# A decoder layer on one core: the chunks for the seven-product trick loaded in three pieces, one of them by an accumulating transfer

## The chip, the cores and the metric

The kernel runs on one core of a Trainium2 chip. TensorE (PE) multiplies, ScalarE (ACT), VectorE (DVE) and GpSimd (POOL) work on tiles in the on-chip memory, SyncE (SP) issues most of the transfers from DRAM, and POOL issues some of its own. Every engine takes its instructions strictly in order. The metric is the device time of one execution in microseconds (us).

## The reference

One decoder layer in float32 for 256 tokens of width 2048:

```python
f = swiglu(rms_norm(h, ffn1_pre_g), w_gate1, w_up1, w_down1); h = h + 0.5 * rms_norm(f, ffn1_post_g)
u = rms_norm(h, mix_pre_g); proj = u @ w_in          # attention branch and Mamba-2 branch, gated, merged
h = h + rms_norm(merged @ w_out, mix_post_g)
f = swiglu(rms_norm(h, ffn2_pre_g), w_gate2, w_up2, w_down2); h = h + 0.5 * rms_norm(f, ffn2_post_g)
# swiglu(x, wg, wu, wd) = (silu(x @ wg) * (x @ wu)) @ wd      width 5632
```

## The kernel before

Every product is made with float32 weights that are split on the chip into a high part (`w_hi`, written by ACT, L124) and a rest (`w_lo`, written by DVE, L125). PE then needs three matmuls for one product (L377 to L379 in the gate and up projections): high by high, high by rest, rest by high. The split tiles have four buffers for the form of 1024 columns and two for that of 512.

The width 5632 of a feed-forward block goes in 11 steps j of 512 columns. In each j, `gate_up` walks through eight pairs of 128 input rows, each a chunk of 1 MB with four blocks of weights. In j = 1 to 10 three of the eight pairs (SP = 2, 4, 6) use a trick with seven products instead of eight, on sums of the weight blocks: these are "sum pairs" here, the others "plain pairs". A plain pair takes 24 matmuls of 512 columns, a sum pair 21. Two feed-forward blocks with ten such j each make 60 sum pairs. The order of the pairs in a j alternates: sum, plain, sum, plain, sum, plain, plain, plain (ORDER), or with a plain pair first (ORDER_D, in each j that follows a down projection).

The class `Ahead` fetches the chunk of a sum pair. Its 1 MB lands in one of two buffers (`raw7`, shared with the tag "h"), and POOL makes four sums of 128x512 in a row (L359): three into a tile `wsum` (e, two buffers, tag "xc") and one back into the chunk. `take` hands chunk and sums to `gate_up`, which splits them in four parts that are named after the code here: **a** (`raw[:, 0:2]`), **b** (`e[:, 0:2]`), **d** (`e[:, 2]`, 512 columns) and **c** (`raw[:, 2:4]`, which holds the fourth sum). Since there are two buffers, a chunk can be fetched only when the chunk two before it has been split.

The program text does not fix the order on an engine. A scheduler orders the instructions by priority, and `tc.high_priority(offset=AHEAD)` around the splits and around the fetch of `Ahead` pulls them forward. So d, which has its own two buffers, stands on ACT ahead of splits of the sum pair before it. SP takes the fetches and the loads of the plain pairs (L393, three buffers) in one queue.

Of the kernel before, what the change touches and what calls it, by code (L numbers as in the profile page):

```python
# [25 lines left out]
ALU = mybir.AluOpType  # L26
AX = mybir.AxisListType

P = 128
# [3 lines left out]
S = 512  # L33
EPS = 1e-6
NFF = FF // S
NP = D // (2 * P)
# [3 lines left out]
AHEAD = 300  # L40
# [12 lines left out]
def decoder_layer(ctx: ExitStack, tc: tile.TileContext, x, x_t, cols, rows, post_g, wgu1, wd1, w_in,  # L53
                  w_in_t, w_dt, w_att, w_ssm, w_out, wgu2, wd2, out):
    nc = tc.nc
# [51 lines left out]
    ahead = [AHEAD]  # L107
# [232 lines left out]
    class Ahead:  # L340
# [4 lines left out]
            self.w, self.units, self.made = w, list(units), []  # L345

        def make(self):
            if self.made or not self.units:
                return
            j, p = self.units.pop(0)  # L350


            raw = hpool.tile([P, 4, S], F32, name="raw7", tag="h")
            e = tmp.tile([P, 3, S], F32, name="wsum", tag="xc", bufs=2)
            with tc.high_priority(offset=AHEAD):
                nc.sync.dma_start(raw, self.w[j, p])
                for o, a, b in ((e[:, 0], raw[:, 0], raw[:, 3]), (e[:, 1], e[:, 0], raw[:, 1]),
                                (e[:, 2], raw[:, 1], raw[:, 3]), (raw[:, 3], e[:, 1], raw[:, 2])):
                    nc.gpsimd.tensor_tensor(out=o, in0=a, in1=b, op=ALU.add)  # L359
            self.made.append((raw, e))  # L360

        def take(self):
            self.make()
            return self.made.pop()

    def gate_up(at, w, j, order, sp, coming, rstd, fetch=None, after={}):


        count = {k: len(sp) for k in ("p1", "p5", "p6", "p7")}
        count.update({k: len(sp) + 2 * (NP - len(sp)) for k in ("g0", "u0", "g1")}, u1=2 * (NP - len(sp)))  # L370
        bank, done = {}, dict.fromkeys(count, 0)

        def prod(k, xh, xl, wh, wl):
            if k not in bank:
                bank[k] = psm.tile([P, S], F32, name="gu", tag="m")
            done[k] += 1
            nc.tensor.matmul(bank[k], xh, wh, start=done[k] == 1, stop=False)  # L377
            nc.tensor.matmul(bank[k], xh, wl, start=False, stop=False)  # L378
            nc.tensor.matmul(bank[k], xl, wh, start=False, stop=done[k] == count[k])  # L379

        new = lambda name: tmp.tile([P, S], F32, name=name, tag="t2")
        units = [i for i, p in enumerate(order) if p in sp]
        c = {}
        for i, p in enumerate(order):
            if p in sp:
                raw, e = coming.take()
            else:
                raw = fetch(p) if fetch else None
                if coming:
                    coming.make()  # L390
                if raw is None:
                    raw = raws.tile([P, 4, S], F32, name="raw")
                    nc.sync.dma_start(raw, w[j, p])  # L393
            sl, k0 = at[p]
            if p in sp:
                ah, al = split(raw[:, 0:2], [P, 2, S])
                bh, bl = split(e[:, 0:2], [P, 2, S])
                dh, dl = split(e[:, 2], [P, S])
                ch, cl = split(raw[:, 2:4], [P, 2, S])
                seq = {"p1": (0, ah[:, 0], al[:, 0]), "u0": (6, ah[:, 1], al[:, 1]),  # L400
                       "p5": (3, bh[:, 0], bl[:, 0]), "p6": (4, bh[:, 1], bl[:, 1]), "p7": (5, dh, dl),
                       "g0": (1, ch[:, 0], cl[:, 0]), "g1": (2, ch[:, 1], cl[:, 1])}
                for k in (("p1", "p5", "p6", "p7", "u0", "g0", "g1") if i == units[0] else
                          ("p1", "u0", "p5", "p6", "p7", "g0", "g1")):
                    f, wh, wl = seq[k]
                    prod(k, sl[:, f, 0], sl[:, f, 1], wh, wl)
            else:
                ah, al = split(raw[:, 0:2], [P, 2, S])
                bh, bl = split(raw[:, 2:4], [P, 2, S])
                for b, (wh, wl) in enumerate(((ah, al), (bh, bl))):  # L410
                    for t in range(NT):
                        for q, kind in enumerate("gu"):
                            k = k0 + (q + b) % 2
                            xh, xl = (sl[:, k, part, t * P:(t + 1) * P] for part in range(2))
                            prod(f"{kind}{t}", xh, xl, wh[:, q], wl[:, q])
            if units and i == units[-1]:
                c = {k: new(f"c_{k}") for k in ("g0", "g1", "u0", "u1")}
                nc.scalar.activation(c["g0"], bank["p1"], AF.Copy)
                u2 = new("u2")
                nc.vector.tensor_tensor(out=u2, in0=bank["p6"], in1=c["g0"], op=ALU.add)  # L420
                nc.vector.tensor_tensor(out=c["g1"], in0=bank["p7"], in1=u2, op=ALU.add)
                nc.vector.tensor_tensor(out=c["u0"], in0=bank["p5"], in1=u2, op=ALU.subtract)
                nc.vector.tensor_tensor(out=c["u1"], in0=bank["p5"], in1=c["g1"], op=ALU.subtract)
            if i in after:
                after[i]()
        out = []
        for t in range(NT):
            g, u = bank[f"g{t}"], bank[f"u{t}"]
            if c:
                nc.vector.tensor_tensor(out=c[f"g{t}"], in0=g, in1=c[f"g{t}"], op=ALU.add)  # L430
                g = c[f"g{t}"]
                nc.vector.tensor_tensor(out=c[f"u{t}"], in0=u, in1=c[f"u{t}"], op=ALU.add)
                u = c[f"u{t}"]
            sg = g if c else new("sg")
            nc.scalar.activation(sg, g, AF.Silu, scale=rstd()[:, t:t + 1])
            nc.vector.scalar_tensor_tensor(out=sg, in0=u, scalar=rstd()[:, t:t + 1], in1=sg,
                                           op0=ALU.mult, op1=ALU.mult)
            out.append(sg)
        return out

    def ffn(xo, scale, wgu, wd, gi, h_of, fetch=None):
# [14 lines left out]
        for a, b in groups:  # L456
            hs = []
            for j in range(a, b):
                if j == 0:
                    steps = dict(scale)  # L460

                    def behind(i):
                        if i in steps:
                            rs.append(steps[i]())
                        if i - 1 in SP:
                            xo.sums(i - 1)
                        if i == NP - 1:
                            coming.make()
                    todo.append(gate_up(xo.at0, wgu, 0, range(NP), (), None, lambda: rs[-1], fetch,
                                        {i: lambda i=i: behind(i) for i in range(NP)}))  # L470
                else:
                    todo.append(gate_up(xo.at, wgu, j, order(j), SP, coming, lambda: rs[-1], after={5: flush}))
            last = b == NFF
            if last:
                h = [hpool.tile([P, D], F32, name=f"h{t}", tag="h") for t in range(NT)]
                for t in range(NT):
                    nc.gpsimd.dma_start(h[t], h_of(t))
            if not post:
                post = PostNorm(gi, 0.5)
                f = post.f  # L480

            def final():
                flush()
                return hs[-1]

            lazy = hs + [final]
            for n in range(4):
                if n == 3:
                    coming.make()
                pd = project(lazy, lambda n, c: wd[n, a + c], n, by_token=2 if last and n == 3 else 0)  # L490
                part = f[:, :, n * S:(n + 1) * S]
                if not last:
                    for t in range(NT):
                        if a == 0:
                            nc.scalar.activation(part[:, t], pd[t], AF.Copy)
                        else:
                            nc.vector.tensor_tensor(out=part[:, t], in0=pd[t], in1=part[:, t], op=ALU.add)
                else:
                    def get(t):
                        v = tmp.tile([P, S], F32, name="fsum", tag="t2")  # L500
                        nc.vector.tensor_tensor(out=v, in0=pd[t], in1=part[:, t], op=ALU.add)  # L501
                        return v
                    post.slab(n, get)
# [21 lines left out]
        return inv_rms(s1)  # L525

    def fetch1(p):
        for k in (2 * p, 2 * p + 1):
            if 2 <= k < NP:
                nc.sync.dma_start(xT[:, k], x_t[k])  # L530
        x1.make(p, xT[:, p], C_PRE1)
        return None if p else raw0
# [450 lines left out]
```

## Time and profile before

| | |
|---|---|
| median of 3 runs | 2853.56 us (2853.48 to 2854.42) |
| profiled execution | 2857.27 us, its span 2855.6 us |
| PE busy | 2785.7 us, 98% of the span |
| DVE, ACT, POOL busy | 1961.6, 1432.6, 542.2 us |
| mean granted clock of PE | 0.996 |
| DMA | 541.50 MB, mean 190 GB/s |

An engine's busy time is the time in which one of its instructions runs, waits inside an instruction included. Consecutive matmuls overlap, so that a matmul of 0.39 us does not mean a step of 0.39 us from one to the next. The span runs from the first to the last instruction.

### The profile page before, as it was taken

What the parts mean: (1) busy time and instruction counts of PE and PEld (TensorE: products, weight loads), DVE (VectorE), ACT (ScalarE), POOL (GpSimd) and SP (SyncE); (2) the same over time, 40 slices, a digit from 0 to 9 for tenths busy, and PEclk for the clock granted to TensorE, in tenths of its full rate; (3) what the DMA queues carried; (4) which work ended last, traced back from release to release, by engine and by line L of the source; (5) the groups of instructions that cost most, each with busy time, mean ns of one, the idle gap of its engine ahead of it and who ended that gap; (6) DMA issues with size and microseconds to landing.
All of it is one profiled execution on the core that took longest, in us unless ns stands there. A gap on an engine that the chain in (4) does not pass through costs nothing. (4 is left out here: it accounts for less than half of the span.)

```text
span 2855.6 us, 33775 instructions
## 1 busy us (share of the span) xinstructions
PE 2785.7 (98%) x13120; PEld 2310.1 (81%) x13120; DVE 1961.6 (69%) x2311; ACT 1432.6 (50%) x1822; POOL 542.2 (19%) x377
## 2 busy tenths in 40 slices
PE   7999999999999999999999999999999999999998
PEld 6887787887788888888788888888877887877877
DVE  6857858867777876777765555545567658678576
ACT  5544544545555555555444444444455545445454
POOL 3403305212012120111100000000033224034030
PEclk9999999999999999999999999999999999999999
DMA  6555555545555555545554445555555554545554
GB/s 239 195 194 184 194 186 193 196 177 213 193 199 178 186 183 184 200 162 193 200 183 171 169 176 178 199 193 197 192 206 192 192 192 177 204 179 192 193 187 165
DMA packets 77985, 541.50 MB, mean 190 GB/s; under 512 B 8768, under 2 KB 8912, under 8 KB 14080
## 3 DMA queue, kind: packets, MB, share of 16 engines
q1 hardware_dynamic: 73152, 519.08, 50.7%
q0 software_dynamic: 4528, 20.09, 2.1%
q8 instruction: 103, 1.69, 0.2%
q14 instruction: 58, 0.48, 0.1%
q10 hardware_dynamic: 144, 0.17, 0.0%
HBM read 532.94 MB, written 6.36 MB: 189 GB/s over the span
## 5 line engine op out<-in xcount | busy, mean ns | idle before, releaser
L125 DVE TENSOR_TENSOR w_lo<-raw,w_hi 128x1024 fp32r<-128x1024 f32 x978 | 1265.0, 1305 | 677.9 <-ACT w_hi L124 670.1
L124 ACT ACTIVATE w_hi<-raw 128x1024 fp32r<-128x1024 f32 x978 | 1022.4, 1057 | 901.1 <-PE acc L132 590.8
L130 PE MATMUL acc<-w_hi,slot 128*128 128x512 f32 x1856 | 729.7, 393 | 1.1 <-DVE y L719 0.3
L131 PE MATMUL acc<-w_lo,slot 128*128 128x512 f32 x1856 | 723.1, 390 | 0.0
L132 PE MATMUL acc<-w_hi,slot 128*128 128x512 f32 x1856 | 720.5, 390 | 0.0
L130 PEld LDWEIGHTS acc<-w_hi,slot 128*128 128x128 f32 x1856 | 348.9, 188 | 78.7 <-ACT slot L187 4.6
L131 PEld LDWEIGHTS acc<-w_lo,slot 128*128 128x128 f32 x1856 | 349.0, 188 | 72.8 <-issue 1.0
L171 PE MATMUL acc<-slot,w_hi 128*128 128x512 f32 x1280 | 407.4, 399 | 0.2 <-ACT zs L763 0.2
L132 PEld LDWEIGHTS acc<-w_hi,slot 128*128 128x128 f32 x1856 | 348.7, 188 | 72.7
L377 PE MATMUL gu<-w_hi,slot 128*128 128x512 f32 x928 | 364.4, 394 | 12.7 <-ACT w_hi L124 12.7
L359 POOL TENSOR_TENSOR wsum<-raw 128x512 f32<-128x512 f32 x120 | 196.1, 1654 | 927.1 <-DMA raw<-in_wgu 743.1
L378 PE MATMUL gu<-w_lo,slot 128*128 128x512 f32 x928 | 364.2, 392 | 5.5 <-DVE w_lo L125 5.5
L379 PE MATMUL gu<-w_hi,slot 128*128 128x512 f32 x928 | 363.3, 391 | 0.0
L173 PEld LDWEIGHTS acc<-slot,w_lo 128*128 128x128 f32 x1280 | 240.4, 188 | 56.3
L124 ACT ACTIVATE w_hi<-wsum 128x512 fp32r<-128x512 f32 (+1 forms) x120 | 101.5, 846 | 309.3 <-POOL wsum L359 260.1
L125 DVE TENSOR_TENSOR w_lo<-wsum,w_hi 128x512 fp32r<-128x512 f32 (+1 forms) x120 | 165.0, 1384 | 127.8 <-ACT w_hi L124 127.8
L173 PE MATMUL acc<-slot,w_lo 128*128 128x256 f32 x1280 | 252.6, 278 | 0.0
L377 PEld LDWEIGHTS gu<-w_hi,slot 128*128 128x128 f32 x928 | 175.7, 189 | 49.9 <-ACT w_hi L124 13.2
L378 PEld LDWEIGHTS gu<-w_lo,slot 128*128 128x128 f32 x928 | 175.7, 189 | 44.1 <-DVE w_lo L125 7.6
L379 PEld LDWEIGHTS gu<-w_hi,slot 128*128 128x128 f32 x928 | 175.5, 189 | 36.5
L171 PEld LDWEIGHTS acc<-slot,w_hi 128*128 128x128 f32 x1280 | 196.4, 189 | 3.8 <-issue 2.4
L378 PE MATMUL gu<-w_lo,sums 128*128 128x512 f32 x420 | 168.7, 402 | 28.2 <-DVE w_lo L125 27.6
(226 smaller groups left out, 2172.5 us busy)
## 6 DMA issues: line engine op xcount, KB each, us to landing
raw<-in_wgu SPq DMA_DIRECT2D x175, 1024.0 KB, 4.8
raw<-in_wd SPq DMA_DIRECT2D x88, 1024.0 KB, 4.8
raw<-in_w_in SPq DMA_DIRECT2D x80, 1024.0 KB, 4.8
raw<-in_w_in_t SPq DMA_DIRECT2D x80, 1024.0 KB, 4.7
raw<-in_w_ssm SPq DMA_DIRECT2D x32, 1024.0 KB, 4.7
raw<-in_w_att SPq DMA_DIRECT2D x16, 1024.0 KB, 4.7
raw<-in_w_out SPq DMA_DIRECT2D x16, 1024.0 KB, 4.7
dec<-acsD POOLq DMA_DIRECT2D x16, 512.0 KB, 5.1
```

Of the source, the lines that this page charges most:

```text
L124: nc.scalar.activation(hi[:, js], raw[:, js], AF.Copy)
L125: nc.vector.tensor_tensor(out=lo[:, js], in0=raw[:, js], in1=hi[:, js].bitcast(F32), op=ALU.subtract)
L130: nc.tensor.matmul(ps, xh, wh, start=first, stop=False)
L131: nc.tensor.matmul(ps, xh, wl, start=False, stop=False)
L132: nc.tensor.matmul(ps, xl, wh, start=False, stop=last)
L171: nc.tensor.matmul(ps[f], hi[:, j, wf[f]], sl[:, j], start=b + j == 0, stop=False)
L173: nc.tensor.matmul(ps[f][:, TT:], lo[:, j, wf[f]], sl[:, j, :TT], start=False, stop=b == len(xs) - 1 and j == 3)
L359: nc.gpsimd.tensor_tensor(out=o, in0=a, in1=b, op=ALU.add)
L377: nc.tensor.matmul(bank[k], xh, wh, start=done[k] == 1, stop=False)
L378: nc.tensor.matmul(bank[k], xh, wl, start=False, stop=False)
L379: nc.tensor.matmul(bank[k], xl, wh, start=False, stop=done[k] == count[k])
```

## The change

A chunk is now fetched in three transfers. SP loads the fourth block twice, side by side, into `e[:, 0:2]` (L357, 512 KB) and the first three blocks into `raw` (L358, 768 KB). POOL then issues a transfer that adds the first two blocks from DRAM onto `e[:, 0:2]` (L359). That makes two of the four sums; the two left are made by POOL as before (L360, L361). The sums in e change places, so that d is now the sum of three blocks and p6 and p7 swap roles. `made` may hold two chunks, `make` is called behind the splits of a sum pair, and the calls elsewhere are moved. The splits of the very first chunk (`fetch1`, p = 0) lose their priority.

```diff
             self.w, self.units, self.made = w, list(units), []
 
         def make(self):
-            if self.made or not self.units:
+            if len(self.made) == 2 or not self.units:
                 return
             j, p = self.units.pop(0)
 
 
             raw = hpool.tile([P, 4, S], F32, name="raw7", tag="h")
             e = tmp.tile([P, 3, S], F32, name="wsum", tag="xc", bufs=2)
+            src = self.w[j, p]
             with tc.high_priority(offset=AHEAD):
-                nc.sync.dma_start(raw, self.w[j, p])
-                for o, a, b in ((e[:, 0], raw[:, 0], raw[:, 3]), (e[:, 1], e[:, 0], raw[:, 1]),
-                                (e[:, 2], raw[:, 1], raw[:, 3]), (raw[:, 3], e[:, 1], raw[:, 2])):
-                    nc.gpsimd.tensor_tensor(out=o, in0=a, in1=b, op=ALU.add)
+                nc.sync.dma_start(e[:, 0:2], src[:, 3:4].broadcast_to([P, 2, S]))
+                nc.sync.dma_start(raw[:, 0:3], src[:, 0:3])
+                nc.gpsimd.dma_start(e[:, 0:2], src[:, 0:2], accum_op=ALU.add)
+                nc.gpsimd.tensor_tensor(out=e[:, 2], in0=e[:, 0], in1=raw[:, 1], op=ALU.add)
+                nc.gpsimd.tensor_tensor(out=raw[:, 3], in0=e[:, 2], in1=raw[:, 2], op=ALU.add)
             self.made.append((raw, e))
 
         def take(self):
             self.make()
-            return self.made.pop()
+            return self.made.pop(0)
...
                 raw = fetch(p) if fetch else None
-                if coming:
-                    coming.make()
                 if raw is None:
...
                 ch, cl = split(raw[:, 2:4], [P, 2, S])
+                coming.make()
                 seq = {"p1": (0, ah[:, 0], al[:, 0]), "u0": (6, ah[:, 1], al[:, 1]),
-                       "p5": (3, bh[:, 0], bl[:, 0]), "p6": (4, bh[:, 1], bl[:, 1]), "p7": (5, dh, dl),
+                       "p5": (3, bh[:, 0], bl[:, 0]), "p7": (5, bh[:, 1], bl[:, 1]), "p6": (4, dh, dl),
                        "g0": (1, ch[:, 0], cl[:, 0]), "g1": (2, ch[:, 1], cl[:, 1])}
-                for k in (("p1", "p5", "p6", "p7", "u0", "g0", "g1") if i == units[0] else
-                          ("p1", "u0", "p5", "p6", "p7", "g0", "g1")):
+                for k in (("p1", "p5", "p7", "p6", "u0", "g0", "g1") if i == units[0] else
+                          ("p1", "u0", "p5", "p7", "p6", "g0", "g1")):
...
-                        if i == NP - 1:
+                        if i >= NP - 2:
                             coming.make()
...
             for n in range(4):
-                if n == 3:
-                    coming.make()
...
     def fetch1(p):
+        ahead[0] = AHEAD if p else 0
```

On ACT, in the first j behind a down projection of the first feed-forward block, before (`raw7_1783` and `wsum_1784` are a chunk and its sums, `wsum_1872` the sums of the next chunk, `raw_1790` and `raw_1878` are plain pairs):

```order
L124 ACTIVATE w_hi_1792<-raw_1790 128x1024
L124 ACTIVATE w_hi_1796<-raw_1790 128x1024
L124 ACTIVATE w_hi_1824<-raw7_1783 128x1024
L124 ACTIVATE w_hi_1828<-wsum_1784 128x1024
L124 ACTIVATE w_hi_1962<-wsum_1872 128x512
L124 ACTIVATE w_hi_1836<-raw7_1783 128x1024
L124 ACTIVATE w_hi_1880<-raw_1878 128x1024
```

The same engine and place with the change (`raw7_1687`/`wsum_1688` and the next chunk's `wsum_1770`):

```order
L124 ACTIVATE w_hi_1799<-raw_1797 128x1024
L124 ACTIVATE w_hi_1803<-raw_1797 128x1024
L124 ACTIVATE w_hi_1831<-raw7_1687 128x1024
L124 ACTIVATE w_hi_1969<-wsum_1770 128x512
L124 ACTIVATE w_hi_1835<-wsum_1688 128x1024
L124 ACTIVATE w_hi_1843<-raw7_1687 128x1024
L124 ACTIVATE w_hi_1887<-raw_1885 128x1024
```

The split d of the next chunk (128x512) stood between b and c of the pair at hand; now it stands between a and b. Over the kernel, d stands directly ahead of b at 1 place before and at 27 with the change, ahead of c at 37 and 12.

On SP, in the same stretch, before:

```order
L356 DMA raw7_1871<-in_wgu1 128x2048
L393 DMA raw_2005<-in_wgu1 128x2048
L356 DMA raw7_1998<-in_wgu1 128x2048
L393 DMA raw_2084<-in_wgu1 128x2048
L393 DMA raw_2172<-in_wgu1 128x2048
```

With the change:

```order
L393 DMA raw_2012<-in_wgu1 128x2048
L357 DMA wsum_1848<-in_wgu1 128x2x512
L358 DMA raw7_1847<-in_wgu1 128x1536
L393 DMA raw_2091<-in_wgu1 128x2048
L393 DMA raw_2179<-in_wgu1 128x2048
```

Each fetch is two entries instead of one, at the same place between the loads of plain pairs (L393). At the very start of the kernel SP had one fetch of 1 MB ahead of the first piece of x; now two L358 (768 KB each) stand there.

On POOL, at the first two chunks, before:

```order
L359 TENSOR_TENSOR wsum_544<-raw7_543 128x512 x2
L359 TENSOR_TENSOR wsum_544<-wsum_544,raw7_543 128x512
L359 TENSOR_TENSOR raw7_543<-wsum_544,raw7_543 128x512
L104 TENSOR_TENSOR pre_rstd_470<-rs_v_471,mhalf_99 128x2
L359 TENSOR_TENSOR wsum_623<-raw7_622 128x512 x2
```

With the change:

```order
L359 DMA wsum_494<-in_wgu1 128x1024
L104 TENSOR_TENSOR pre_rstd_477<-rs_v_478,mhalf_99 128x2
L360 TENSOR_TENSOR wsum_494<-wsum_494,raw7_493 128x512
L361 TENSOR_TENSOR raw7_493<-wsum_494,raw7_493 128x512
L359 DMA wsum_523<-in_wgu1 128x1024
```

The power that makes the scale of x (`pre_rstd`) stood behind the four sums of the second chunk; now it stands behind the issue of the second accumulating transfer, and the two sums left come after it.

## Rows read from the trace of the kernel before

**Rows 1.** Page: busy us, share of the span, instructions.
```profile
PE 2785.7 (98%) x13120; PEld 2310.1 (81%) x13120; DVE 1961.6 (69%) x2311; ACT 1432.6 (50%) x1822; POOL 542.2 (19%) x377
```
**Rows 2.** Waits of PE: engine, waited for, us in total, times, longest.
```profile
PE gu L378 <- DVE w_lo L125: 33.1, 37, 2.5
```
**Rows 3.** Waits of all engines, same columns.
```profile
POOL wsum L359 <- DMA raw<-in_wgu: 743.1, 50, 84.6
...
ACT w_hi L124 <- POOL wsum L359: 260.1, 59, 5.6
```
**Rows 4.** Timeline of one fetch: start us, us, engine, operation, [idle before].
```profile
238.84 0.33 SPq L356 DMA_DIRECT2D raw<-in_wgu  x1
...
243.90 2.52 POOL L359 TENSOR_TENSOR wsum<-raw 128x512 f32<-128x512 f32 x2 [6.22 <-DMA raw<-in_wgu]
...
246.46 0.64 ACT L124 ACTIVATE w_hi<-wsum 128x512 fp32r<-128x512 f32 x1 [4.75 <-POOL wsum L359]
247.00 2.00 ACT L124 ACTIVATE w_hi<-raw 128x1024 fp32r<-128x1024 f32 x2
247.13 1.10 DVE L125 TENSOR_TENSOR w_lo<-wsum,w_hi 128x512 fp32r<-128x512 f32 x1 [3.82 <-ACT w_hi L124]
...
248.16 4.59 DVE L125 TENSOR_TENSOR w_lo<-raw,w_hi 128x1024 fp32r<-128x1024 f32 x3
...
250.54 0.33 SPq L356 DMA_DIRECT2D raw<-in_wgu  x1
```
**Rows 5.** Timeline of PE early on, two matmuls six apart.
```profile
19.08 0.39 PE L378 MATMUL gu<-w_lo,slot 128*128 128x512 f32 x1
...
20.44 0.39 PE L378 MATMUL gu<-w_lo,slot 128*128 128x512 f32 x1
```
**Rows 6.** Timeline of PE: three of its waits in one group of j.
```profile
250.53 0.50 PE L378 MATMUL gu<-w_lo,sums 128*128 128x512 f32 x1 [0.91 <-DVE w_lo L125]
...
279.38 0.50 PE L378 MATMUL gu<-w_lo,sums 128*128 128x512 f32 x1 [1.60 <-DVE w_lo L125]
290.84 0.50 PE L378 MATMUL gu<-w_lo,sums 128*128 128x512 f32 x1 [0.94 <-DVE w_lo L125]
```
**Rows 7.** Timeline of PE: its waits at the two feed-forward blocks' starts.
```profile
12.25 1.29 PE L377 MATMUL gu<-w_hi,slot 128*128 128x512 f32 x2 [12.25 <-ACT w_hi L124]
...
40.62 0.50 PE L378 MATMUL gu<-w_lo,slot 128*128 128x512 f32 x1 [1.54 <-DVE w_lo L125]
...
68.45 0.50 PE L377 MATMUL gu<-w_hi,sums 128*128 128x512 f32 x1 [2.04 <-ACT sg L435]
...
2139.30 0.50 PE L378 MATMUL gu<-w_lo,slot 128*128 128x512 f32 x1 [1.02 <-DVE w_lo L125]
...
2144.86 0.80 PE L378 MATMUL gu<-w_lo,slot 128*128 128x512 f32 x1 [2.50 <-DVE w_lo L125]
```
**Rows 8.** Transfers: issuing queue, count, KB each, median us from issue to landing.
```profile
raw<-in_wgu SPq DMA_DIRECT2D x175, 1024.0 KB, 4.8
...
dec<-acsD POOLq DMA_DIRECT2D x16, 512.0 KB, 5.1
...
out<-h SPq DMA_DIRECT2D x8, 256.0 KB, 2.2
```
**Rows 9.** The 16 transfers of 512 KB that POOL issues at L694.
```profile
L694 POOL DMA_DIRECT2D dec<-acsD x16: 547/564/686, 842.4 to 1358.0; - x16
...
DMA to landing us min/median/max: 3.7/5.1/6.1
```
**Rows 10.** Source line L359, POOL: count, duration ns min/median/max, first and last start.
```profile
L359 POOL TENSOR_TENSOR wsum<-raw x120: 1272/1300/4334, 30.4 to 2766.6; 128x512 f32<-128x512 f32 x120
```
**Rows 11.** Source line L125, DVE, same columns.
```profile
L125 DVE TENSOR_TENSOR w_lo<-raw,w_hi x978: 1204/1225/3436, 12.2 to 2837.8; 128x1024 fp32r<-128x1024 f32 x196
```
**Rows 12.** Stretches: us; PE, PEld, DVE, ACT, POOL busy (x); PEclk, DMA share, GB/s.
```profile
69.50:73.00 3.50, 3.50 (x10) 2.71 (x9) 3.50 (x3) 2.66 (x4) 3.42 (x3) 0.51 0.23 33
...
2144.80:2148.30 3.50, 3.44 (x8) 2.78 (x9) 3.50 (x5) 0.75 (x1) 0.00 (x0) 0.51 0.67 225
```

## The prediction

> **What bounds the kernel now.** I read the page first: PE is busy for 2785.7 of 2855.6 us, so everything the kernel can win is the 70 us in which PE sits idle [rows 1]. Then the waits of PE: apart from the start, the one large item is the matmul that waits for a `w_lo`, 33.1 us in 37 waits [rows 2]. Following that back through the waits of all engines: DVE waits for ACT, and ACT's 260.1 us of waiting for POOL's sums, 59 times, is what holds it up; POOL itself mostly waits for the chunk to land [rows 3]. So the chain of one fetch is what matters, and the timeline has it [rows 4]. SP issues a fetch at 238.84; the sums begin at 243.90; ACT, which stood at split d of that chunk, goes on at 246.46, 7.62 us after the issue. Only then come c of the pair at hand (ACT 247.00), d's rest (DVE 247.13) and c's rest (248.16), and the buffer that this frees lets SP issue the next fetch at 250.54. The reader is to see a loop: fetch, sum, split, free the buffer, fetch. It takes 250.54 - 238.84 = 11.70 us, of which DVE and ACT have 4.08.
>
> PE's work in such a turn is a sum pair and a plain pair, 21 + 24 = 45 matmuls. Six matmuls take 20.44 - 19.08 = 1.36 us, 0.227 each [rows 5], so 10.2 us. The loop is 1.5 us longer than the work, and PE waits 0.91 at 250.53 [rows 6]. A waiting matmul also hides 0.39 - 0.227 = 0.16 of its wait, so PE loses 1.07; the other 0.43 come out of splits made ahead. At 279.38 and 290.84 the same [rows 6]. At the starts of the two blocks lie 1.54 + 1.02 + 2.50 = 5.06 of the 33.1 [rows 7]; in the steady j remain 28.0 us in 34 waits, with the hidden 34 x 0.16 = 5.5 about 33 us.
>
> **The change, part by part.** *Two pairs ahead* frees nothing: the chunk has two buffers before and after, the fetch before already goes out when the chunk two before it is split, and SP's order shows the fetches at the same places. I cost it at 0. What changes is the loop.
>
> (1) The fetch becomes a chain of two transfers. The 512 KB of L357 have no row on SP's queue: 256 KB out take 2.2 and 1 MB in takes 4.8 [rows 8], I take the middle, 3.6 with the wake-up of POOL. Then POOL issues the accumulating transfer and it lands after L. No such transfer is in the trace. The nearest rows are POOL's 512 KB of L694: 3.7 at least, 5.1 in the median, 6.1 at most [rows 9]. Below nothing the cost of adding can't be, so 3.7 is the lower end; at the upper end the destination is read as well, 512 KB more, which between 256 KB and 1 MB costs (4.8 - 2.2) / 1.5 = 1.7, so 7.8. L694's transfers go in twos, and the second has 512 KB of its twin in front of it, about what the second read would be: between median and maximum, L = 5.6.
>
> (2) One sum instead of two before d: 1.3 [rows 10]. The sums removed, 2 x 60 x 1.3 = 156 us of POOL, are off PE's path except through this place, and against them stand 60 issues of 0.56 [rows 9].
>
> (3) On ACT d now stands ahead of b at 27 places, not of c. The wait at d so holds up b, which PE needs earlier, and b frees `e` for the next L357. From d to that: d's step 247.00 - 246.46 = 0.54, b's high part 1.05 (two such take 2.00 at 247.00), its rest 1.21 [rows 4, 11], and 0.25 for d's rest on DVE in between: 3.05.
>
> The loop with the change is 3.6 + L + 1.3 + 3.05 = 8.0 + L, with 0.05 for two wake-ups. Against 10.2 us of work and 0.43 in hand PE loses L - 2.6 a turn, 3.0 at L = 5.6. I count one full turn in each of the 20 j with sums, and the other 7 places (the second in a j behind a down projection, whose loop has already stretched) at a third: 22.3 turns. That gives 22.3 x 3.0 = 67 us of waiting where 33 are now: +34.
>
> (4) At the starts. The two L358 ahead of x are 512 KB more than the one fetch before, by the same slope 1.7 us later than 12.25 [rows 7]: +1.7; between nothing, if they are passed in the queues, and 2.4. The first splits without priority stand behind two short slot instructions that run while the chunk is still under way: 0. The wait at 68.45 for the scale of x stays: POOL has the power behind the second accumulating issue now, which itself waits for an L357, instead of behind four sums. At the second block's start, 1.02 and 2.50 should go, since POOL has half the sums to make there, and with them the stretch after it in which PE's clock is granted at 0.51 for 3.4 us [rows 12], worth half of that, 1.7: -5.2. Together -3.5.
>
> (5) The DMA queues carry 0.75 MB more for each of 60 chunks, 45 MB on 541.5: the plain pairs' loads have three buffers and I cost it at 0; if that cover goes, a late load costs PE up to the 2.4 us that L357 and L358 occupy longer.
>
> Sum: +34 - 3.5 = +30 us. On the profiled execution's 2857.3 that is 2888; the median of the runs is 3.7 lower, so 2884. With L in between, 22.3 x (L - 2.6) - 36.5: -12 at 3.7, +19 at 5.1, +42 at 6.1, +80 at 7.8.
>
> The Trainium skill, "Collectives: The Full Stack", section "The bandwidth ceiling: the fold count and why AG ≠ RS ≠ AR", says that an add in a DMA engine costs no cycles of its own but needs two source reads on one ring, so such a stream runs at half the rate (1.93 measured there). No run here shows it yet. By that rule the full 1.7 come on top of the median, L = 6.8, and the sum would be +57, 2911.
>
> **The rivals.** *Faster.* The accumulating transfer lands like a lone plain one. For it: the smallest of L694 is 3.7, and its firsts have no twin ahead. Against it: the median is 5.1, and a destination must be read. From L = 4.2 down the sum above is negative. What makes more of it is DVE: POOL's sums slow it, as where d's rest takes 1.10 and three of c's kind take 4.59 instead of 3 x 1.21 [rows 4, 11], and half of them go. At most all steady waits vanish, -33 - 3.5; at L = 3.7 the sum alone gives -12. The middle, -24: 2830.
>
> The Trainium skill, "SBUF — State Buffer", section "Who interferes with whom", has a VectorE instruction with two SBUF inputs and a GpSimd instruction that reads SBUF block each other for whole instructions. The trace agrees: the 4.59 are about 1.0 more than three rests, near one sum's 1.3. By it this rival has its price; the sum above counts only 0.25 of it.
>
> *Clock.* The waits of 2.04 and 2.50 [rows 7] are each followed by 3.5 us at a granted 0.51 [rows 12], that is 1.2 GHz instead of 2.4; 1.60 at 279.38 is not. If 20 waits of about 3 us each bring such a stretch, 20 x 1.7 = 34 come on top: 2918.
>
> *Nothing.* SP's order and the buffers are as before, L lies near 4.2 and the longer chain and the shorter sums cancel: 2854.
>
> **How the numbers follow.** About 0.2% or 5.7 us is what a measurement of this kernel can tell from no change. Forecast, 0.45: 2884, its own range 2866 to 2908 (L from 4.9 to 6.5). Clock or an L near 7: 0.15, 2918. Nothing: 0.08. Faster: 0.32, 2830. So faster 0.32, same 0.08, slower 0.60. The range from 2826 to 2924 leaves out about 1 in 10 at each end.
>
> **What would show it.** L359's time to landing is the first thing to read: 5.6 for the forecast, under 4.2 for the faster rival. Then L357 to L357 across an alternating pair (13.6 against 11.70), ACT's waits for POOL's sums (more than 260.1 us), PE's waits for `w_lo` (about 60 us against 33.1, at 20 to 27 places and near 3 us long), granted clock behind them, first matmul at 13.9. The prediction is wrong if L359 lands fast, if d ends up off the path because b was split long before PE needs it, or if the plain pairs' loads come late beside the accumulating ones.

## The result, and the profile after

The changed kernel takes 3029.5 us (median of 4 runs, 3020.5 to 3035.4) against 2853.7 for the kernel before: ratio 1.0611, 95% interval 1.0598 to 1.0624. It is slower by 176 us. The sign was forecast; 2884 and its range, up to 2924, were far too low.

The page after (busy us, share, instructions; then the DMA queues: packets, MB, share of 16 engines):

```profile
PE 2848.1 (94%) x13120; PEld 2349.2 (78%) x13120; DVE 1873.3 (62%) x2311; ACT 1429.2 (47%) x1822; POOL 365.0 (12%) x317
...
q1 hardware_dynamic: 89472, 534.81, 49.6%
q0 software_dynamic: 13168, 51.55, 7.9%
```

The span is 3028.9 us, 173.3 longer than before. PE's time splits exactly into busy and idle: it is busy 62.4 us longer with the same 13120 matmuls [rows 1], and idle for 180.8 instead of 69.9, 110.9 more. DVE, ACT and POOL are busy for less time than before, so the work of no other engine explains it. The waits (engine, waited for: us, times, longest):

```profile
ACT w_hi L124 <- POOL wsum L360: 448.6, 60, 12.3
POOL wsum L360 <- DMA wsum<-in_wgu: 303.2, 47, 10.4
PE gu L379 <- ACT w_hi L124: 120.1, 33, 14.0
PE gu L380 <- DVE w_lo L125: 32.6, 38, 1.5
PE gu L379 <- ACT sg L436: 6.2, 2, 5.7
```

Without the first matmul's 14.0, PE waits 144.9 us here; before it was 33.1 [rows 2] and some small ones. ACT's 260.1 us at split d [rows 3] have become 448.6. One fetch, to be laid beside [rows 4] (timeline: start us, us, engine, operation, idle before):

```profile
252.67 0.38 SPq L357 DMA_DIRECT2D wsum<-in_wgu  x1
253.77 0.33 SPq L358 DMA_DIRECT2D raw<-in_wgu  x1
...
256.04 0.33 SPq L393 DMA_DIRECT2D raw<-in_wgu  x1
...
257.83 0.87 POOL L359 DMA_DIRECT2D wsum<-in_wgu  x1 [6.91 <-DMA wsum<-in_wgu]
265.53 1.25 POOL L360 TENSOR_TENSOR wsum<-wsum,raw 128x512 f32<-128x512 f32 x1 [6.83 <-DMA wsum<-in_wgu]
266.81 1.58 ACT L124 ACTIVATE w_hi<-wsum 128x512 fp32r<-128x512 f32 x2 [11.41 <-POOL wsum L360]
...
268.44 0.79 PE L379 MATMUL gu<-w_hi,sums 128*128 128x512 f32 x1 [5.30 <-ACT w_hi L124]
...
269.88 0.38 SPq L357 DMA_DIRECT2D wsum<-in_wgu  x1
```

From fetch to fetch 17.21 us instead of 11.70. It reads: 5.16 until POOL issues the accumulating transfer, 7.70 until its landing lets POOL add, 1.28 for the sum, 3.07 for d, b and the freeing of the buffer. ACT stands 11.41 us at d, and b, which PE needs, stands behind it (the x2 at 266.81 is d and b together). PE then waits, and this is what its clock does (stretch; busy us of PE, PEld, DVE, ACT, POOL; granted clock; DMA share; GB/s):

```profile
258.00:265.90 7.90, 5.14 (x23) 3.94 (x21) 0.00 (x0) 0.00 (x0) 1.07 (x2) 1.00 0.79 214
265.90:272.80 6.90, 3.72 (x8) 2.64 (x9) 5.32 (x5) 5.29 (x7) 2.15 (x2) 0.51 0.19 64
272.80:283.00 10.20, 10.03 (x44) 7.93 (x43) 2.24 (x3) 0.67 (x1) 0.98 (x2) 1.00 0.83 240
```

PE has stood since 263.15; from 265.90 it is granted half, 1.2 GHz, the wait of 5.30 ends at 268.44, and work goes on at half speed until 272.80. There are 30 such stretches between the first matmul and the last, 181 us in all; before there were 5, 20.5 us. The transfers (count, KB, median us to landing), with L359's issue and landing in full:

```profile
raw<-in_wgu SPq DMA_DIRECT2D x115, 1024.0 KB, 6.0
...
raw<-in_wgu SPq DMA_DIRECT2D x60, 768.0 KB, 5.2
wsum<-in_wgu SPq DMA_DIRECT2D x60, 512.0 KB, 4.4
wsum<-in_wgu POOLq DMA_DIRECT2D x60, 512.0 KB, 7.0
```
```profile
L359 POOL DMA_DIRECT2D wsum<-in_wgu x60: 847/872/915, 34.9 to 2934.5; - x60
...
DMA to landing us min/median/max: 5.2/7.0/11.2
```

The accumulating transfer lands after 7.0 in the median, not 5.6, and the plain 1 MB loads beside it need 6.0 where they needed 4.8 [rows 8].

The 7.0 is the median of two groups. When 25 of the 60 transfers were issued, a 1 MB load of a plain pair (L393) was on its way, as at 256.04 above; these landed after 7.0 to 11.2, in the median 7.8. The other 35 took 5.5 in the median. PE waits 22 times for more than 2 us at a `w_hi` after the start, and the transfer in front of each of these waits is one of the 25.

### The profile page after: what moved, and what is told of

Read it like the earlier page. It is cut to its first block, busy times and chain, and to the rows that moved or that the text cites. A ratio compares the mean times of both kernels' runs of the same rounds, so it can differ in the third digit from the quotient of the medians.

```text
span 3028.9 us, 33954 instructions
## 1 busy us (share of the span) xinstructions
PE 2848.1 (94%) x13120; PEld 2349.2 (78%) x13120; DVE 1873.3 (62%) x2311; ACT 1429.2 (47%) x1822; POOL 365.0 (12%) x317
## 3 DMA queue, kind: packets, MB, share of 16 engines
q0 software_dynamic: 13168, 51.55, 7.9%
## 5 line engine op out<-in xcount | busy, mean ns | idle before, releaser
L125 DVE TENSOR_TENSOR w_lo<-raw,w_hi 128x1024 fp32r<-128x1024 f32 x978 | 1214.5, 1253 | 688.4 <-ACT w_hi L124 681.2
L379 PE MATMUL gu<-w_hi,slot 128*128 128x512 f32 x928 | 375.0, 405 | 33.5 <-ACT w_hi L124 33.5
L380 PE MATMUL gu<-w_lo,slot 128*128 128x512 f32 x928 | 374.6, 404 | 11.3 <-DVE w_lo L125 11.3
L381 PE MATMUL gu<-w_hi,slot 128*128 128x512 f32 x928 | 372.5, 402 | 0.0
L125 DVE TENSOR_TENSOR w_lo<-wsum,w_hi 128x1024 fp32r<-128x1024 f32 (+1 forms) x120 | 139.9, 1182 | 369.1 <-ACT w_hi L124 369.1
L124 ACT ACTIVATE w_hi<-wsum 128x1024 fp32r<-128x1024 f32 (+1 forms) x120 | 98.5, 841 | 486.2 <-POOL wsum L360 448.6
L379 PE MATMUL gu<-w_hi,sums 128*128 128x512 f32 x420 | 180.6, 430 | 92.7 <-ACT w_hi L124 86.5
L379 PEld LDWEIGHTS gu<-w_hi,slot 128*128 128x128 f32 x928 | 182.1, 196 | 75.5 <-ACT w_hi L124 36.9
L381 PEld LDWEIGHTS gu<-w_hi,slot 128*128 128x128 f32 x928 | 181.5, 196 | 38.9
L380 PE MATMUL gu<-w_lo,sums 128*128 128x512 f32 x420 | 180.0, 429 | 21.4 <-DVE w_lo L125 21.3
```

The lines of the kernel that those rows point to most:

```text
L124: nc.scalar.activation(hi[:, js], raw[:, js], AF.Copy)
L125: nc.vector.tensor_tensor(out=lo[:, js], in0=raw[:, js], in1=hi[:, js].bitcast(F32), op=ALU.subtract)
```

## The experiments

Theory A was: ACT stops at split d of the next chunk; b of the chunk at hand, the buffer that b frees and the next fetch stand behind it; so the whole length of one fetch lies in a loop, and each microsecond that the chain of two transfers adds is paid, with the clock on top. The rivals: the traffic or the software queue (POOL's, which carries L359) holds everything up wherever d stands; or other parts of the change do it. Names in the diffs are those of the changed kernel.

| run | what is different | median us | PE busy | PE idle |
|---|---|---|---|---|
| before | | 2853.7 | 2785.7 | 69.9 |
| x5_before_sums | before's fetch and sums; two ahead, first splits | 2854.7 | 2784.0 | 70.4 |
| x1_pool_sums | the same, sums in the new form | 2881.4 | 2794.5 | 83.8 |
| x2_plain_second | chain of two, no add | 2946.7 | 2819.5 | 113.6 |
| changed kernel | chain of two, add | 3029.5 | 2848.1 | 180.8 |
| x3_d_behind_b | changed, d behind its own b | 2805.9 | 2767.4 | 36.5 |

(Medians; the kernel before has medians between 2853.7 and 2856.4 beside these runs. Busy and idle are of one profiled execution each; that of x2 is the fastest of its runs.)

**Undoing the accumulating transfer**, in two forms:

```diff
-nc.sync.dma_start(e[:, 0:2], src[:, 3:4].broadcast_to([P, 2, S]))
-nc.sync.dma_start(raw[:, 0:3], src[:, 0:3])
-nc.gpsimd.dma_start(e[:, 0:2], src[:, 0:2], accum_op=ALU.add)
+nc.sync.dma_start(raw, src)
 # x1: e0 = r0+r3, e1 = r1+r3, e2 = e0+r1, r3 = e2+r2
 # x5: e0 = r0+r3, e1 = e0+r1, e2 = r1+r3, r3 = e1+r2; p6, p7 as before
```

> The changed kernel with the accumulating transfer undone: one fetch of 1 MB and four sums on POOL again; two chunks ahead, first splits without priority and the order of p5, p7, p6 stay. Theory A (the loss of 176 us is the longer chain of a fetch, L357, L359, L360, that ACT stands and waits for at split d): the time is back within 15 us of before, 2840 to 2870, ACT's waits for POOL's sums near 260 us, PE's near 33 to 45, a landing of the 1 MB at 4.8 us. Theory B (two chunks ahead, the new order of the sums or the first splits cost it): it stays above 2930.

Measured: 2881.4 us, 1.0089 [1.0074, 1.0104], 349.0 us of ACT's waits for POOL. Neither theory's number. The timeline of x1 shows why:

```profile
244.70 2.53 POOL L360 TENSOR_TENSOR wsum<-raw 128x512 f32<-128x512 f32 x2 [6.63 <-DMA raw<-in_wgu]
247.19 1.29 POOL L360 TENSOR_TENSOR wsum<-wsum,raw 128x512 f32<-128x512 f32 x1
248.51 0.63 ACT L124 ACTIVATE w_hi<-wsum 128x512 fp32r<-128x512 f32 x1 [6.13 <-POOL wsum L360]
```

Split d takes `e2`, which the new formula makes of `e0`; on POOL it is the third sum, and ACT goes on at 248.51 when it has ended. In the kernel before d's sum needs the raw chunk alone, stands second, and ACT goes on at 246.46 while POOL begins the third [rows 4]. So the run still had a change in it that I had overlooked. x5 took it out.

> The 1 MB fetch and the four sums on POOL word for word as in the kernel before (d is there the sum of chunks 1 and 3, ready as POOL's second, not third), with p6 and p7 as before; of the change only two chunks ahead and the first splits without priority are left. Theory A: the 27 us that the run with four sums in the new form lost are the third sum, 1.3 us, that d waits for in each loop; without it the time is that of before, 2848 to 2862. Rival (two chunks ahead or the first splits cost the 27): 2875 or more.

Measured: 2854.7 us, 1.0002 [0.9992, 1.0011], as theory A had it. Two chunks ahead and the first splits without priority are together worth nothing here, and one POOL sum of 1.3 us more in front of d costs 27 us.

**The chain without the add.**

```diff
-nc.gpsimd.dma_start(e[:, 0:2], src[:, 0:2], accum_op=ALU.add)
+nc.gpsimd.dma_start(e[:, 0:2], src[:, 0:2])
```

> The changed kernel with L359 as a plain transfer, which overwrites what L357 brought instead of adding to it (so two of the four sums of weights are left out); queue, size, chain and all waits are the same. Theory A with the add's second read as its main price: L359's time to landing falls from 7.0 in the median to 4.5 to 5.5, the loop from 17.2 to about 14.5, the time to 2870 to 2930. If the two reads are all of it: 2860 or less. If the software queue and the chain of two transfers are the price and not the add: L359 still lands at 6.5 or more and the time stays above 2990.

Measured: 2946.7 us, 1.0321 [1.0303, 1.0338]; landing 3.3/4.9/7.8, issue 570 ns. L fell as the theory with the second read had it; the time stayed 17 us above that theory's range, which ended at 2930. One tight turn, that is, one in which a fetch waits for the one before it:

```profile
238.01 0.38 SPq L357 DMA_DIRECT2D wsum<-in_wgu  x1
...
243.18 0.57 POOL L359 DMA_DIRECT2D wsum<-in_wgu  x1 [6.91 <-DMA wsum<-in_wgu]
249.34 1.26 POOL L360 TENSOR_TENSOR wsum<-wsum,raw 128x512 f32<-128x512 f32 x1 [5.59 <-DMA wsum<-in_wgu]
250.63 1.58 ACT L124 ACTIVATE w_hi<-wsum 128x512 fp32r<-128x512 f32 x2 [8.63 <-POOL wsum L360]
...
253.70 0.38 SPq L357 DMA_DIRECT2D wsum<-in_wgu  x1
```

15.69 us, and 6.16 of them for a plain transfer: here too the 26 transfers that were issued with an L393 under way took longer, 6.1 in the median against 4.2 for the other 34. So of the 176 us, 92 come with the chain of two plain transfers (x2 against x5) and 83 with the add. The 27 us of x1 are no part of them: in the changed kernel one sum stands before d, not three.

**Less traffic beside the chain.**

```diff
-nc.sync.dma_start(raw[:, 0:3], src[:, 0:3])
+nc.sync.dma_start(raw[:, 1], src[:, 1])        # splits a and c and the last sum read raw[:, 1] for 0 and 2
```

> The changed kernel, order and chain unchanged, with less traffic beside the chain: L358 brings 256 KB (chunk 1 alone) instead of 768, and the splits a and c read chunk 1 where they would read chunks 0 and 2, so those weights are left out. Theory: 1.6 us of the 17.2 us loop are L357 sharing the DMA engines with L358, and part of L359's 7.6 the same, which the prediction costed at nothing. Then the POOL issue stands at about 4.2 after L357 instead of 5.2, L359 lands in 6 to 6.5 in the median, a loop of 15 to 16, the time 2930 to 2985. Rival (the landing is long by itself, the neighbours do nothing): 3015 or more, L359 still near 7.0.

Measured: 2979.1 us, 1.0430 [1.0415, 1.0446], 50 less than the changed kernel and inside the theory's range; L359 lands after 5.1/6.2/10.1, POOL's issue follows L357 by 4.57 in the median instead of 4.97. So the 512 KB that L358 no longer brings are a part of the price; 123 us of the loss remain, with the loads of the plain pairs still beside the chain.

**The accumulating transfer in halves.**

```diff
-nc.gpsimd.dma_start(e[:, 0:2], src[:, 0:2], accum_op=ALU.add)
+for k in range(2):
+    nc.gpsimd.dma_start(e[:, k], src[:, k], accum_op=ALU.add)
```

> The changed kernel with L359 cut into two accumulating transfers of 256 KB, one for each half; d needs the first only. If the price goes by bytes read and added (7.0 us in the median for 512 KB, 4.9 without the add): the first half lands after 4.5 to 5.5, the loop loses about 2 us, time 2920 to 2980. If it is a fixed price for each transfer, or the traffic around it: the first lands after 6.5 or more, the second issue of 0.9 us comes on top, time 3030 or more.

Measured: 3002.7 us, 1.0518 [1.0502, 1.0534], between the two. The 256 KB land after 3.6/6.7/11.0, the firsts of the pairs after 6.2 in the median, and each is issued in 0.98 us. Half the bytes are far from half the time. Of the 60 firsts, the 30 that were issued with a load of a plain pair under way took 6.5 in the median, the others 3.9; for the whole 512 KB these were 7.8 and 5.5. So the half, too, is long where such a load is under way.

**Split d behind split b of the same chunk.** The order of ACT before the edit reads a8 d9 b8 c8 in such a place (pairs numbered), after it a8 b8 d8 c8.

```diff
-dh, dl = split(e[:, 2], [P, S])
+dh, dl = split(e[:, 2], [P, S], behind=last[0])     # last[0]: b's ACTIVATE
...
-            for i in queue.pop(0) if queue else ():
+            for i in [behind] if behind else queue.pop(0) if queue else ():
                 st.enter_context(tc.issue_after(i.ins))
...
-                nc.scalar.activation(hi[:, js], raw[:, js], AF.Copy)
+                last[0] = nc.scalar.activation(hi[:, js], raw[:, js], AF.Copy)
```

> The changed kernel, accumulating transfer and all, with one thing moved: split d of a chunk is issued behind split b of the same chunk instead of one pair ahead. Theory A (ACT stands at d of the next chunk, and behind it wait b of the chunk at hand, the buffer that b frees, and so the next fetch): one fetch no longer waits for the one before, the 17.2 us loop opens, ACT's waits for POOL's sums fall from 448.6 to under 150, PE's waits at w_hi from 120.1 to under 30, half-speed stretches from 188 us to under 40, and the time falls below 2860, by the work alone perhaps to 2815. Rival (the traffic: 45 MB more and a queue whose packets take twice as long hold up every load, wherever d stands): it stays above 2930. L359 should take its 7 us in both.

Measured: 2805.9 us, 0.9827 [0.9813, 0.9842] of the kernel before, 224 us less than the changed kernel, with every transfer, sum and matmul of it in place. L359's landing is 5.3/7.1/10.9: as slow as ever, and harmless. ACT's waits for that sum are 0.5 us in all, PE's idle time is 36.5, and 10 us are left at half speed.

```profile
ACT w_hi L125 <- POOL wsum L361: 0.5, 2, 0.2
```

The timeline of x3 (its L358, L360, L361 are L357, L359, L360 of the changed kernel):

```profile
250.87 1.58 ACT L125 ACTIVATE w_hi<-wsum 128x1024 fp32r<-128x1024 f32 x2 [1.65 <-PE gu L382]
...
253.87 0.38 SPq L358 DMA_DIRECT2D wsum<-in_wgu  x1
...
258.13 0.87 POOL L360 DMA_DIRECT2D wsum<-in_wgu  x1 [0.87 <-DMA wsum<-in_wgu]
...
261.12 1.58 ACT L125 ACTIVATE w_hi<-wsum 128x1024 fp32r<-128x1024 f32 x2 [0.35 <-PE gu L382]
...
264.68 0.38 SPq L358 DMA_DIRECT2D wsum<-in_wgu  x1
265.35 1.98 POOL L361 TENSOR_TENSOR wsum<-wsum,raw 128x512 f32<-128x512 f32 x1 [6.34 <-DMA wsum<-in_wgu]
```

ACT now waits for PE at b and d, not for POOL, and the second fetch goes out at 264.68, before the sum of the first at 265.35: two fetches are under way, 10.8 us apart, about the work of a turn. The rival of traffic alone is out.

> The kernel before, with the same one thing moved: split d behind split b of its own chunk. By theory A the loop of 11.70 us opens here as well and most of the 33 us at w_lo go, with the clock's slow stretches behind them: 2820 to 2840. By the rival, that the 11.70 us loop was bound by POOL's four sums and DVE beside them and not by d's place, no change within 8 us: 2846 to 2862.

Measured: 2823.6 us, 0.9889 [0.9875, 0.9904]: the same edit of d on the kernel before takes ACT's 260.1 us [rows 3] to 12.1 and PE's wait of 33.1 [rows 2] to 8.0.

```profile
ACT w_hi L125 <- POOL wsum L360: 12.1, 11, 1.1
...
PE gu L379 <- DVE w_lo L126: 8.0, 7, 1.3
PE gu L378 <- ACT sg L436: 3.1, 1, 3.1
```

So x3's accumulating transfer, once no wait of ACT hangs on it, gains 18 us over x4's four sums. A part of it is DVE's, whose second parts are shorter (mean ns of one after the comma, x3 first, x4 below): PE's 8.0 us at `w_lo` are 0.8 in x3. The wait of 3.1 above, which is for the scale of x, and one of 1.5 near the start are gone too, and 10 us at half speed instead of 20 are left; against that x3's first matmul comes 2.3 us later.

```profile
L126 DVE TENSOR_TENSOR w_lo<-raw,w_hi 128x1024 fp32r<-128x1024 f32 x978 | 1269.7, 1304 | 757.3 <-ACT w_hi L125 749.3 <-PE tp L208 4.7
```
```profile
L126 DVE TENSOR_TENSOR w_lo<-raw,w_hi 128x1024 fp32r<-128x1024 f32 x978 | 1331.2, 1370 | 676.3 <-ACT w_hi L125 668.8 <-PE tp L208 4.7
```

**What L is worth there**: x3 without the add, and x3 with two adds (L360 is L359 of the changed kernel).

```diff
-nc.gpsimd.dma_start(e[:, 0:2], src[:, 0:2], accum_op=ALU.add)
+nc.gpsimd.dma_start(e[:, 0:2], src[:, 0:2])                         # x7
+for k in range(2):                                                  # x10
+    nc.gpsimd.dma_start(e[:, 0:2], src[:, 0:2], accum_op=ALU.add)
```

> The accumulating kernel with d behind b, but L359 plain: it overwrites instead of adding, so two sums of weights are left out. Theory A (with d behind b no fetch waits for the one before, and the transfer has time to spare): L359 lands at about 4.9 instead of 7.1 and the time stays within 5 us of 2806. If the landing still decides: 20 us or more faster, below 2786.

Measured: 2804.9 us, 1.0 less than x3, with L359 at 3.4/4.7/9.1 instead of 7.1. Whether the transfer adds makes no difference there that these runs can tell.

> The accumulating kernel with d behind b, with L359 issued twice in a row on the same tile (so two sums of weights take chunks 0 and 1 twice). How much time to spare the fetch has there: with two landings of 7 and two issues of 0.9 the chain from L357 to the sums is 5.2 + 15 + 2.6 = 23 against two turns of 10.2, 20.4, so POOL's sums should come late at the tight places by some 2 to 4 us and the time should rise by 20 to 80 us, 2826 to 2886. If the accumulating transfer has plenty of room there: within 5 us of 2806. If every turn waits again as in the changed kernel: 3000 or more.

Measured: 3040.3 us, 1.0644 [1.0626, 1.0661]. I expected 2826 to 2886, and missed. POOL's timeline:

```profile
258.11 1.29 POOL L362 TENSOR_TENSOR wsum<-wsum,raw 128x512 f32<-128x512 f32 x1 [8.70 <-DMA wsum<-in_wgu]
...
259.48 2.15 POOL L363 TENSOR_TENSOR raw<-wsum,raw 128x512 f32<-128x512 f32 x1
261.58 0.86 POOL L361 DMA_DIRECT2D wsum<-in_wgu  x1
...
267.69 0.86 POOL L361 DMA_DIRECT2D wsum<-in_wgu  x1 [5.25 <-DMA wsum<-in_wgu]
...
277.71 1.26 POOL L362 TENSOR_TENSOR wsum<-wsum,raw 128x512 f32<-128x512 f32 x1 [9.16 <-DMA wsum<-in_wgu]
```

I had counted two turns for the fetch. But the second transfer adds onto what the first brought and waits for its landing (5.25 us at 267.69), and POOL issues them, stands at the sum that needs them, and has the next chunk's transfers behind that sum. On POOL only one is under way at a time, in a loop of 277.71 - 258.11 = 19.6 us. In x3 the same loop is 7.1 + 1.4 to 2.0 + 1.3 to 2.2, some 10 to 11, just the work of a turn. By this sum the transfer is off the path by a small margin, not by 10 us.

**The best version.** x3, with the first two chunks of the first block fetched without priority:

```diff
-with tc.high_priority(offset=AHEAD):
+# self.n: the number of units at the start
+with tc.high_priority(offset=AHEAD) if len(self.units) < self.n - 2 or self.w is wgu2 else nullcontext():
```

> The accumulating kernel with d behind b, and the fetches of the first two chunks of the first block without priority, so that L358 stands behind the loads of x and of the first weights on SP's queue instead of ahead of them. First matmul at 10 to 12 us instead of 13.85, and the time 2 to 4 us lower, 2802 to 2804, if nothing comes late behind it. If the first chunk then lands late for its splits at the start of j = 1: 2806 or more.

Measured: 2799.8 us (2798.8 to 2800.8), 0.9810 [0.9795, 0.9825], better than both kernels and 2 us below what I expected. The first matmul comes earlier than that, too:

```profile
7.44 1.22 PE L381 MATMUL gu<-w_hi,slot 128*128 128x512 f32 x2 [7.44 <-ACT w_hi L125]
```

## Why the prediction was right in its mechanism and wrong in its size

**Two pairs ahead and the first splits.** They were forecast to be worth nothing, and that was right: x5 has 1.0002.

**The loop.** The steps were the right ones, and (2) and (3) have their size: the sum 1.28 for 1.3, d to the next fetch 3.07 for 3.05. That d ahead of b makes the fetch a loop is shown by x3. Wrong are the two transfers: 5.16 for 3.6 until POOL's issue, 7.70 for 5.65 with the wake-up. This turn takes 17.2 instead of 13.6. Turns of 16.9 to 17.4 come only seven times; the sum is better checked on all waits. PE waits 138.7 us at `w_hi` and `w_lo` after the start (120.1 + 32.6 - 14.0), 22 times for more than 2 us. So the count of 22.3 turns was about right, and a turn cost 6.2 us (138.7 / 22.3) instead of 3.0. And the waits came at `w_hi`: those at `w_lo`, which were to rise to about 60, stayed at 32.6.

The step that failed is the size of the two transfers. L was taken from the 16 transfers of L694, and L357 from transfers of other sizes [rows 8, 9]. For a transfer with no load of a plain pair under way L was right, 5.5 for 5.6; at the 22 places that count such a load had been issued 0.3 to 3.2 us before L359, and L was 7.0 to 11.2, in the median 7.7. Term (5), the 45 MB more, was costed at 0 because the plain pairs have buffers (its limit of 2.4 us is not worked out from any row); that the loads would slow the chain itself I did not ask. x9 takes 31 MB away and gains 50 us. The add is the other part: without it (x2) the median is 4.9 instead of 7.0, and the issue 570 instead of 872 ns.

Packets show the add by itself. Of the 13168 packets of POOL's queue 8640 are L359's; the other 4528 took 2.1% of 16 x 2855.6, 959 us, in the kernel before. In x2 the queue has these packets too:

```profile
q0 software_dynamic: 13168, 51.55, 5.1%
```

5.1% of 16 x 2933.1 are 2393 us, 166 ns for one packet of L359; with the add 7.9% of 16 x 3028.9 are 3829, 332 ns, twice as long. The Trainium skill, "Collectives: The Full Stack", section "The bandwidth ceiling: the fold count and why AG ≠ RS ≠ AR", has the add of a reducing collective cost a second source read and half the rate. The trace agrees, 332 against 166 ns. By that rule L was 6.8 and the time 2911 in the prediction; the median of 7.0 is near it, and the time still far above, since what lay beside it was missing.

**The clock.** The prediction held it as a rival with 0.15, with 20 stretches that cost 1.7 us each, 34 in all; it belonged in the sum. PE's busy time is up by 62.4 us. There are 30 half-speed stretches, and most are 6.8 us long, not 3.5. Not only the waits near 5 us brought such a length: the four of 2.7 to 3.1 us, each with a shorter one 0.5 us behind it, did so too. So the rival was too small even for the 3 us waits of the forecast. That it was held apart from them, where 2.04 and 2.50 had already brought one stretch each [rows 7, 12], is the second failing step.

**The starts.** First matmul 14.02 for 13.9. At the second block's start no wait for `w_lo` is left, as forecast. The wait that was put down to the scale of x did not stay at 2.04 [rows 7] but is 5.74, and it is no longer a wait for the scale:

```profile
62.78 1.05 POOL L104 TENSOR_TENSOR pre_rstd<-rs_v,mhalf 128x2 f32<-128x2 f32 x1
...
72.56 0.63 ACT L124 ACTIVATE w_hi<-wsum 128x512 fp32r<-128x512 f32 x1 [5.89 <-POOL wsum L360]
73.10 0.67 ACT L436 ACTIVATE sg<-gu,pre_rstd 128x512 f32<-128x512 f32 x1
...
73.82 0.80 PE L379 MATMUL gu<-w_hi,sums 128*128 128x512 f32 x1 [5.74 <-ACT sg L436]
```

POOL has the power done at 63.83. ACT stands at a split d for 5.89 us, and the second `sg`, for which PE waits, stands behind that split. It is the mechanism of the loop once more, at a place where I had not looked for it; in x3 the wait is gone.

**The account.** PE is idle 110.9 us longer: 105 at `w_hi` and `w_lo` (138.7 against 33.1 and a few tenths), 4 at this `sg` and 2 before the first matmul. It is busy 62.4 us longer: the half-speed stretches hold 139.6 us of PE's busy time instead of 18.2, and half of the difference is 61. The forecast had 34 for the waits, -3.5 for the starts and nothing for the clock.

**The rivals.** *Faster* held the right thing about DVE, in the wrong place: the second parts are quicker with half of POOL's sums, but DVE was not what PE waited for. The Trainium skill, "SBUF — State Buffer", section "Who interferes with whom", lets two-input DVE instructions and POOL's reads exclude each other. x3 and x4 agree (1304 against 1370 ns, DVE busy 1910.8 against 2029.1). Once d is out of the way the change pays 18 us, of which about 7 are waits for DVE. *Nothing* is out.

**What stays open.** That a load of a plain pair makes L359 longer is read from which transfers were long, in the changed kernel, in x2 and in x6; no run takes these loads away. And the 92 us of the chain without the add are explained by one loop (15.69 against 11.70), not by a run that separates queue and traffic.

## What to carry to other kernels

Before a fetch is made longer, look for what is queued behind the instruction that waits for it: here one early split on ACT held up the split that frees the buffer for the next fetch, and moving it was worth more (31 us on the kernel before, 224 on the changed one) than the new form of the sums (18 us, x3 against x4). A transfer in such a loop is to be sized by the rows in which its neighbours are in flight too, and a wait of PE that comes back every turn gets the price of the slower clock in the sum, not in a rival. The accumulating transfer pays here (18 us) once no engine stands waiting for it, and on the queue that issues it only one is under way, since its sum stands behind it.

## What the runs showed of the hardware

An accumulating transfer of 512 KB from DRAM into SBUF landed after 5.2/7.0/11.2 us, the same without the add after 3.3/4.9/7.8; POOL needs 872 ns to issue it instead of 570, and 976 ns for one of half the size. Issued with a 1 MB load under way it took 7.8 in the median, otherwise 5.5; the plain one 6.1 and 4.2. The 1 MB loads beside it landed in 6.0 instead of 4.8. In the gate and up projections of the changed kernel PE's 21 waits of 2.7 to 6.2 us each brought 6.8 us at half speed (one of them 10.2); its waits of 2.05 and 2.38 us, each with a shorter one behind it, brought 3.4.
